# A branch on the last expert's token count picks a float32 or a split program

## The chip, the cores and the metric

The kernel runs on one core of a Trainium2 chip, in one launch. The metric is the device time in microseconds (us); three runs of the kernel before gave 1691.51, 1692.79 and 1695.13 us, median 1692.79. One more execution was profiled; the profile gives the span of that execution's instructions and the work of each engine: TensorE (PE, with its weight loads as PEld), VectorE (DVE), ScalarE (ACT), GpSimd (POOL) and SyncE (SP, whose queue issues most transfers). A "q" behind a name is that engine's instruction queue (sequencer).

## The reference, cut to what matters

Two layers of a token backbone. The first layer ends in a dense channel mixer; the second, which the change concerns, ends in a mixture of eight experts for 256 tokens of width 1024, two experts per token, hidden width 3584:

```python
def swiglu(h, w1, w3, w2):
    return (jax.nn.silu(h @ w1) * (h @ w3)) @ w2

logits = (xt @ router_w).astype(jnp.float32) + router_b.astype(jnp.float32)
top_val, top_idx = lax.top_k(logits, TOP_K)          # TOP_K = 2
gates = jax.nn.softmax(top_val, axis=-1)
# each token's row goes through its two experts:
#   out[token] += gate * swiglu(x[token], w1[e], w3[e], w2[e])
```

Then follow a gated residual, `xl + g2 * f`, and a final RMSNorm with a gain row `final_g`. All values are float32. The weights of one expert are 3 x 1024 x 3584 numbers, 42 tiles of 1 MB each; every expert's weights are read once.

## The kernel before, in words

**Places.** The eight experts are run one after the other, in eight places numbered 0 to 7. Expert 0 is always in place 0. The others are ordered at run time by their token counts (`keys`, `ranks`, `places`, lines 1204 to 1218): `RANK = (0, 7, 1, 6, 2, 5, 3, 4)` (line 823) says which rank of the order, counted from the largest, comes to which place. So place 1 has the expert with the fewest tokens, place 2 the one with the most, and place 7, the last, the one of rank 4.

**Two programs for a place.** Places in `NAT = (1, 3, 5)` run in plain float32 with room for 64 tokens: `up_nat`, `flip_nat`, `down_nat`, `scatter_nat` (lines 1341 to 1399). A 1 MB weight tile is used as it landed, and its slot is free when the last matmul that reads it has ended. All other places, the last among them, have room for 128 tokens and run split: each half tile (a chunk of 128 x 1024) is cast to a high part on ScalarE (line 135) and its remainder is made on VectorE (line 136); a product is three matmuls (`mm3`, lines 243 to 245) of high and low parts. There the slot is free when both halves have been split. The functions are `up`, `flip`, `down`, `scatter` (lines 1401 to 1465). Tokens beyond a place's room are done at the end, in a loop under the test `rv > 0` (lines 1575 to 1604), which is skipped where there are none.

**Slices.** A place has seven slices of 512 hidden columns. `up` makes silu(h w1) * (h w3), `flip` transposes it, `down` multiplies by w2 into accumulators that live through the place. The loop (lines 1516 to 1535) runs `up` of slice g, then `lower` (the `down`) of slice g - 1, then `flip` of slice g, so TensorE has other work while ScalarE and VectorE prepare the flipped operand. This holds across the border of two places too.

**Weights.** `plan` (lines 835 to 843) lists all tiles in the order of use. `w_dma` issues the next one on SP's queue as soon as a slot is free; by the time of the experts twelve slots of 1 MB rotate (four from line 90, the others added at lines 1043 to 1153). For a place whose expert is known only at run time, SP reads its number into a register first (line 1252). `w_split(n)` splits chunks ahead of use, up to five ahead; a count in `HOLD` can hold the last ones back.

**Order by hand.** The order of instructions on each engine is the order of the program text. Small work is set between by `agenda`: `plan_late(fs, at)` puts functions at numbered steps, and each weight chunk (split) or pair of weight blocks (float32) pops one step. So the routing (`gates`) runs in the first slices of place 0; `fetch`, the gather of the next place's tokens, runs inside the place before it; `scatter`, which weights a place's result by its gates and by the residual's gate row `G[1]` and adds it to the tokens, runs inside the place after it.

**The end.** In the last slice `up` has an argument `mid`: `down` of slice 54 is run between its w1 and its w3 product, and the w3 tiles come last but one in `plan`. All remaining chunks are then split, and `warm` fills TensorE with small products of ones while it waits (lines 1529 to 1538). The last scatter, the squares for the final norm (`ends`, ScalarE), the product with the gain row (POOL), the overflow test and the final scaling follow.

Of the kernel before, what the change touches and what calls it, by code (L numbers as in the profile page):

```python
# [12 lines left out]
OP = mybir.AluOpType  # L13
AX = mybir.AxisListType

P = 128
# [18 lines left out]
def tile_hybrid_headgroup_dit_moe(ctx: ExitStack, tc: tile.TileContext, a, out: bass.AP):  # L35
# [51 lines left out]
    HOLD = [0]  # L87
# [30 lines left out]
    def w_split(n):  # L118
        while st["split"] < min(n, len(chunks) - HOLD[0]):
# [701 lines left out]

    NAT = (1, 3, 5)
# [12 lines left out]
    for g in range(LAST + 2):  # L835
        if g <= LAST:
            p_moe("moe_w1", g)
            if g < LAST:
                p_moe("moe_w3", g)
        if g:  # L840
            p_moe("moe_w2", g - 1)
        if g == LAST:
            p_moe("moe_w3", g)
# [337 lines left out]
    eidx = ti[:, 8:16]  # L1181
# [4 lines left out]
    def gates():  # L1186
# [50 lines left out]
        later = [keys, ranks, places, numbers] + [lambda t=t: pick(posp[:, t], pos[:, t]) for t in range(2)] \  # L1237
# [30 lines left out]
    sn = [fa(4096 + 512 + i * 256, 256) for i in range(2)]  # L1268
    hidn = [fa(oT + 2048 + i * 256, 256) for i in range(2)]

    def gather(e, o):
        if e in NAT:
# [105 lines left out]
    def scatter_nat(ya, v, g):  # L1378
        yh, yl = ra(HS, 512), ra(HS + 512, 512)

        def weigh(hf):
            hp = slice(64 * hf, 64 * hf + 64)
            nc.vector.scalar_tensor_tensor(ya[hp], ya[hp], g[hp], G[1][hp, 512 * hf:512 * hf + 512], op0=OP.mult, op1=OP.mult)
        r = [lambda: weigh(0), lambda: weigh(1), lambda: nc.scalar.copy(yh, ya), lambda: nc.vector.tensor_sub(yl, ya, yh)]
# [16 lines left out]
    def up(e, i, h, nxt, mid=None):  # L1401
        b1, b3 = bank(), bank()
        for w, b in (("moe_w1", b1), ("moe_w3", b3)):
# [6 lines left out]
            if w == "moe_w1":  # L1410
                s = sbuf[i % 2]
                nc.scalar.activation(s, b1, AF.Silu)
                if mid is not None:
                    mid()
                    HOLD[0] = 3
# [54 lines left out]
    def fetch(e):  # L1470
        o = one_hot(e)

        def hot():
            for t, c in enumerate(list(place(e))[0]):
                if e in NAT:
# [4 lines left out]
        return [hot] + gather(e, o)  # L1480

    w_more(ra(4096, 1024), ra(5120, 1024))
    first = fetch(0)
# [5 lines left out]
    plan_late(gates(), range(2, 22))  # L1489
# [7 lines left out]
    SCAT_N = [2, 2, 6, 6, 14, 15, 18, 19, 34, 35, 38, 39]  # L1497
    ya = {}

    def lower(g):  # L1500
        e1, i1 = divmod(g, NSL)
        if i1 == 0:
            ya[e1] = bank("acc") if e1 in NAT else [bank("acc") for _ in range(2)]
        if e1 in NAT:
# [5 lines left out]
        if i1 == NSL - 1 and e1 in NAT:  # L1510
            plan_late(scatter_nat(ya.pop(e1), *sl[0]), SCAT_N)
        elif i1 == NSL - 1:
            plan_late(scatter(ya.pop(e1), *sl[0], *([HG] if g == LAST else [])),
                      SCAT if g < LAST else [0, 1, 2, 4, 5, 4, 6, 1, 2, 3, 5, 8, 6, 9])
    sl = [None]
    for g in range(LAST + 1):
        e, i = divmod(g, NSL)
        if i == 0 and e + 1 < NE:
            plan_late(fetch(e + 1), GATH if e else GATH_1)
        if e in NAT:  # L1520
            s = up_nat(e, i)
        else:
            s = up(e, i, hg[e], moe_next, (lambda: lower(g - 1)) if g == LAST else None)
        if 0 < g < LAST:
            lower(g - 1)
        if g == 0:
            plan_late([lambda s=s: hts.update({0: flip(0, s)})], [3])
        else:
            if g == LAST:
                HOLD[0] = 2  # L1530
                w_split(len(chunks))
                warm(4)
            hts[g] = flip_nat(g, s) if e in NAT else flip(g, s)
            if e in NAT and i == NSL - 1:
                w_split(st["use"] + NW[0])
    warm(7)
    HOLD[0] = 0
    lower(LAST)
# [150 lines left out]
```

## Time and profile before

| | |
|---|---|
| median of three runs | 1692.79 us (1691.51 to 1695.13) |
| the profiled execution, its time | 1693.55 us |
| its span | 1691.7 us |
| PE busy | 1636.0 us (97%), 8876 matmuls |
| DVE busy | 1147.1 us (68%) |
| ACT busy | 902.9 us (53%) |
| POOL busy | 26.2 us (2%) |
| data moved | 492.02 MB, mean 291 GB/s |
| weight tiles of the experts | 336 of 1024 KB, on SP's queue |

Rows of groups read: line of the kernel, engine, operation, what it writes and reads with its shape, how often, then busy time and the mean of one in ns, then the engine's idle time before them and what ended it. Rows of a timeline read: start in us from the span's start, duration, engine, line, operation, shapes, and in brackets the idle time before it with what ended it. Durations of matmuls overlap, since they are pipelined: the distance from start to start is what one costs. Rows of a single line read: line, engine, operation, count, then shortest, median and longest duration in ns, then the first and the last start.

### The profile page before, as it was taken

What the parts mean: (1) busy time and instruction counts of PE and PEld (TensorE: products, weight loads), DVE (VectorE), ACT (ScalarE), POOL (GpSimd) and SP (SyncE); (2) the same over time, 40 slices, a digit from 0 to 9 for tenths busy, and PEclk for the clock granted to TensorE, in tenths of its full rate; (3) what the DMA queues carried; (4) which work ended last, traced back from release to release, by engine and by line L of the source; (5) the groups of instructions that cost most, each with busy time, mean ns of one, the idle gap of its engine ahead of it and who ended that gap; (6) DMA issues with size and microseconds to landing.
All of it is one profiled execution on the core that took longest, in us unless ns stands there. A gap on an engine that the chain in (4) does not pass through costs nothing. (4 is left out here: it accounts for less than half of the span.)

```text
span 1691.7 us, 23644 instructions
## 1 busy us (share of the span) xinstructions
PE 1636.0 (97%) x8876; PEld 1268.6 (75%) x8876; DVE 1147.1 (68%) x1790; ACT 902.9 (53%) x1269; POOL 26.2 (2%) x54
## 2 busy tenths in 40 slices
PE   7999999999999999999999999999999999999996
PEld 5786788888888887978786568875588755788885
DVE  3784589966545799568983159841498513889996
ACT  4456555222225654568773157731477413777874
POOL 0101000000000010000000000000000000000001
PEclk9999899999999999999999999999999999999998
DMA  9645334665665555346999999999999999999980
GB/s 360 219 150 177 113 125 153 241 233 219 215 232 175 174 206 182 142 168 230 346 355 385 420 421 421 413 370 422 421 420 409 367 422 421 421 416 370 362 311 27
DMA packets 69226, 492.02 MB, mean 291 GB/s; under 512 B 7984, under 2 KB 8752, under 8 KB 9712
## 3 DMA queue, kind: packets, MB, share of 16 engines
q1 hardware_dynamic: 67856, 486.97, 73.8%
q0 software_dynamic: 816, 2.72, 0.7%
q8 instruction: 72, 1.18, 0.3%
q10 hardware_dynamic: 432, 0.74, 0.1%
q14 instruction: 50, 0.41, 0.1%
HBM read 489.36 MB, written 1.05 MB: 290 GB/s over the span
## 5 line engine op out<-in xcount | busy, mean ns | idle before, releaser
L136 DVE TENSOR_TENSOR RA<-FA,RA 128x1024 fp32r<-128x1024 f32 x572 | 685.2, 1226 | 157.9 <-ACT RA L135 151.6
L135 ACT CAST RA<-FA 128x1024 fp32r<-128x1024 f32 x572 | 590.7, 1051 | 278.1 <-PE mm L245 165.1
L243 PE MATMUL mm<-RA 128*128 128x512 f32 (+1 forms) x1200 | 458.6, 383 | 10.3 <-ACT RA L135 4.4
L244 PE MATMUL mm<-RA 128*128 128x512 f32 (+1 forms) x1200 | 451.7, 377 | 5.1 <-DVE RA L136 3.6
L245 PE MATMUL mm<-RA 128*128 128x512 f32 (+1 forms) x1200 | 450.6, 376 | 0.0
L243 PEld LDWEIGHTS mm<-RA 128*128 128x128 f32 x1200 | 226.9, 189 | 57.2 <-ACT RA L893 5.2
L244 PEld LDWEIGHTS mm<-RA 128*128 128x128 f32 x1200 | 227.5, 190 | 47.2 <-DVE RA L136 5.9
L245 PEld LDWEIGHTS mm<-RA 128*128 128x128 f32 x1200 | 227.2, 189 | 41.0
L243 PE MATMUL acc<-RA 128*128 128x512 f32 (+1 forms) x664 | 252.1, 380 | 3.9 <-DVE RA L765 1.8
L245 PE MATMUL acc<-RA 128*128 128x512 f32 (+1 forms) x664 | 248.0, 374 | 0.0
L244 PE MATMUL acc<-RA 128*128 128x512 f32 (+1 forms) x664 | 247.8, 373 | 0.0
L1349 PE MATMUL mm<-FA 128*64 128x256 f32 x1344 | 155.0, 382 | 0.0
L243 PEld LDWEIGHTS acc<-RA 128*128 128x128 f32 x664 | 125.5, 189 | 30.0 <-issue 3.8
L245 PEld LDWEIGHTS acc<-RA 128*128 128x128 f32 x664 | 125.3, 189 | 22.4 <-issue 0.3
L244 PEld LDWEIGHTS acc<-RA 128*128 128x128 f32 x664 | 125.6, 189 | 20.4 <-issue 0.2
L1349 PEld LDWEIGHTS mm<-FA 128*64 128x64 f32 x1344 | 92.5, 137 | 50.6 <-issue 6.8
L310 DVE SCALAR_TENSOR_TENSOR FA<-FA 128x1024 f32<-128x1024 f32 x80 | 94.5, 1222 | 7.9 <-DMA FA<-in_w_modt_dram 7.8
L1297 DVE TENSOR_TENSOR RA<-lc,RA 128x128 fp32r<-128x128 f32 x40 | 11.5, 291 | 121.7 <-ACT RA L1294 121.7
L1372 PE MATMUL acc<-FA 128*64 128x512 f32 x336 | 78.5, 597 | 0.0
L476 DVE SCALAR_TENSOR_TENSOR FA<-FA,pv 128x512 f32<-128x512 f32 (+1 forms) x128 | 74.2, 615 | 1.3 <-ACT FA L472 0.8
L1293 ACT ACTIVATE lc<-mm,modT 128x128 f32<-128x128 f32 x40 | 18.4, 460 | 84.5 <-PE mm L1288 84.5
L764 ACT CAST RA<-FA 128x256 fp32r<-128x256 f32 x44 | 17.9, 408 | 58.7 <-PE acc L245 55.9
(261 smaller groups left out, 1132.4 us busy)
## 6 DMA issues: line engine op xcount, KB each, us to landing
FA<-in_moe_w_dram SPq DMA_DIRECT2D x336, 1024.0 KB, 9.7
FA<-in_w_modt_dram SPq DMA_DIRECT2D x28, 1024.0 KB, 4.9
FA<-in_ffn_dram SPq DMA_DIRECT2D x22, 1024.0 KB, 4.8
FA<-in_ffn_w_dram SPq DMA_DIRECT2D x22, 1024.0 KB, 4.9
FA<-in_w_mod_dram SPq DMA_DIRECT2D x20, 1024.0 KB, 6.9
FA<-in_w_in_dram SPq DMA_DIRECT2D x20, 1024.0 KB, 5.0
FA<-in_w_out_dram SPq DMA_DIRECT2D x12, 1024.0 KB, 4.8
FA<-in_x_dram SPq DMA_DIRECT2D x2, 1024.0 KB, 8.6
```

The lines of the kernel that those rows point to most:

```text
L135: nc.scalar.copy(wh, raw)
L136: nc.vector.tensor_sub(wl, raw, wh)
L243: nc.tensor.matmul(ps, ll, rh, start=start, stop=False, skip_group_check=True)
L244: nc.tensor.matmul(ps, lh, rl, start=False, stop=False, skip_group_check=True)
L245: nc.tensor.matmul(ps, lh, rh, start=False, stop=stop, skip_group_check=True)
L310: nc.vector.scalar_tensor_tensor(o, raw[:, c], 1.0, csb[:, s], op0=OP.mult, op1=OP.mult, accum_out=modT[l][:, 2 * r + c, s:s + 1])
L476: nc.vector.scalar_tensor_tensor(acc, src, w, acc, op0=OP.mult, op1=OP.add)
L764: nc.scalar.copy(hh, hid(s, f))
L1293: nc.scalar.activation(v["h32"], v["b"], AF.Identity, scale=sc, bias=bi)
L1297: nc.vector.tensor_sub(h.l[:, k], v["h32"], h.h[:, k])
L1349: nc.tensor.matmul(b[64 * c:64 * c + 64, 0:256], hn[:, k], raw[:, q, 256 * c:256 * c + 256], start=k == 0, stop=k == 7, skip_group_check=True)
L1372: nc.tensor.matmul(ya[64 * hf:64 * hf + 64, :], hid[:, jj * P + 64 * r:jj * P + 64 * r + 64], raw[:, 2 * hf + jj], start=i == 0 and r == 0 ...
```

## The change

The last expert is taken out of the loop and written twice. A register is loaded with its token count, `last_n`; where it is over 64 the split program runs, otherwise a float32 program like that of places 1, 3 and 5. Both programs begin with the scatter of place 6 and end with the squares of the final norm. To make that possible:

- the place before it, place 6, gathers the last expert's tokens twice, in the split form (now at steps 9 to 38) and in the float32 form (steps 49 to 78);
- splitting stops at the last chunk of place 6 (`LIM`), so that nothing of the last expert is prepared before the branch; its transfers are still issued into free slots by `w_dma`;
- `down` of place 6's last slice is run before the branch, directly behind its own `flip`, and its w2 tiles come before the last expert's w1 tiles in `plan`;
- `HOLD`, `mid` and the `warm` calls of the last slice are gone; the last slice is a slice like the others;
- the halves of the gate row `G[1]` that float32 places need are copied once, in the routing (`gate_halves`), and `scatter_nat` weights all 128 partitions in one operation instead of two;
- the load of the final gain row is issued inside each program.

The bookkeeping of the program text (`state`, `back`) is saved ahead of the first program and restored ahead of the second.

```diff
-    HOLD = [0]
+    LIM = [None]
     def w_split(n):
-        while st["split"] < min(n, len(chunks) - HOLD[0]):
+        while st["split"] < min(n, len(chunks) if LIM[0] is None else LIM[0]):
...
     for g in range(LAST + 2):
         if g <= LAST:
...
+            ws = [("moe_w1", g), ("moe_w3", g), ("moe_w2", g - 1)]
+            if g == (NE - 1) * NSL:
+                ws = ws[2:] + ws[:2]
+            for w, h in ws:
+                if h >= 0:
+                    p_moe(w, h)
...
+            nc.vector.tensor_copy(last_n, over[:, NE - 1:NE])
...
+        def gate_halves():
+            for hf in range(2):
+                hp = slice(64 * hf, 64 * hf + 64)
+                nc.scalar.copy(gn[hp], G[1][hp, 512 * hf:512 * hf + 512])
-        later = [keys, ranks, places, numbers] + ...
+        later = [gate_halves, keys, ranks, places, numbers] + ...
...
     def raw_tile(key):
-        j = raw_j.pop(0)
+        if key[1] == NE - 1:
+            j = chunks[st["use"]][0]
+            st["use"] += 2
+        else:
+            j = raw_j.pop(0)
...
-        r = [lambda: weigh(0), lambda: weigh(1), lambda: nc.scalar.copy(yh, ya), lambda: nc.vector.tensor_sub(yl, ya, yh)]
+        r = [lambda: nc.vector.scalar_tensor_tensor(ya, ya, g, gn, op0=OP.mult, op1=OP.mult), lambda: nc.scalar.copy(yh, ya), lambda: nc.vector.tensor_sub(yl, ya, yh)]
...
+    def body(g, nat):
+        e, i = divmod(g, NSL)
+        s = up_nat(e, i) if nat else up(e, i, hg[e], moe_next)
+        if g and g - 1 in hts:
+            lower(g - 1, nat if i else e - 1 in NAT)
+        if g == 0:
+            plan_late([lambda: hts.update({0: flip(0, s)})], [3])
+        else:
+            hts[g] = flip_nat(g, s) if nat else flip(g, s)
+
     sl = [None]
-    for g in range(LAST + 1):
+    LIM[0] = [plan[j][0][1] == NE - 1 and plan[j][0][0].startswith("moe") for j, _ in chunks].index(True)
+    for g in range((NE - 1) * NSL):
         e, i = divmod(g, NSL)
+        if i == 0:
+            if e < NE - 2:
+                plan_late(fetch(e + 1, e + 1 in NAT), GATH if e else GATH_1)
+            else:
+                plan_late(fetch(e + 1, False), [0] + [9 + 4 * k + d for k in range(KD) for d in (0, 1, 1)])
+                plan_late(fetch(e + 1, True), [45] + [49 + 4 * k + d for k in range(KD) for d in (0, 1, 1)])
+        body(g, e in NAT)
+        if e in NAT and i == NSL - 1:
+            w_split(st["use"] + NW[0])
+    lower((NE - 1) * NSL - 1, False)
+    for fs in agenda:
+        run(fs)
+    del agenda[:]
...
+    def last_place(nat):
+        assert st["use"] == LIM[0] == st["split"]
+        scat(NE - 2, False)
+        if not nat:
+            LIM[0] = None
+            run(fetch(NE - 1, False)[:1])
+            w_split(st["use"] + NW[0])
+        for i in range(NSL):
+            body((NE - 1) * NSL + i, nat)
+        lower(LAST, nat)
+        nc.gpsimd.dma_start(fg, a["final_g"].to_broadcast([P, D]))
+
+        at = [0, 1, 2, 3, 4, 3, 5, 3, 6, 3, 7] if nat else [0, 1, 2, 3, 4, 3, 5, 1, 2, 3, 4, 6, 5, 7]
+        plan_late(scatter_nat(ya[NE - 1], *sl[0]) if nat else scatter(ya[NE - 1], *sl[0], HG), at)
+        plan_late([lambda t=t, hf=hf: ends(t, hf) for hf in range(2) for t in range(2)], [4, 5, 6, 7])
+        for fs in agenda:
+            run(fs)
+        del agenda[:]
...
+    ln = nc.values_load(last_n[0:1, 0:1], min_val=0, max_val=256)
+    saved, limit = state(), LIM[0]
+    with tc.If(ln > 64) as cmp:
+        last_place(False)
+    back(saved)
+    LIM[0] = limit
+    with cmp.Else():
+        last_place(True)
```

More of the change, by code (lines that the diff above doesn't have):

```diff
@@ L1236, in counts @@
             nc.vector.tensor_copy(cmax, cm)
-        later = [keys, ranks, places, numbers] + [lambda t=t: pick(posp[:, t], pos[:, t]) for t in range(2)] \
+        def gate_halves():
+            for hf in range(2):
+                hp = slice(64 * hf, 64 * hf + 64)
+                nc.scalar.copy(gn[hp], G[1][hp, 512 * hf:512 * hf + 512])
+        later = [gate_halves, keys, ranks, places, numbers] + [lambda t=t: pick(posp[:, t], pos[:, t]) for t in range(2)] \
             + [lambda t=t: pick(gtp[:, t], gt[:, t]) for t in range(2)] + [counts]
@@ L1268, in tile_hybrid_headgroup_dit_moe, with gather @@
     sn = [fa(4096 + 512 + i * 256, 256) for i in range(2)]
+    gn = fa(oT + 2560, 512)
     hidn = [fa(oT + 2048 + i * 256, 256) for i in range(2)]
-    def gather(e, o):
-        if e in NAT:
+    def gather(e, o, nat=False):
+        if nat:
             def product(k):
@@ L1468, in one_hot, with fetch @@
         return oh[e % 2]
-    def fetch(e):
+    def fetch(e, nat):
         o = one_hot(e)
@@ L1479, in hot @@
                     nc.vector.tensor_scalar(o[t], iota[:, 0:P], c, None, op0=OP.is_equal)
-        return [hot] + gather(e, o)
+        return [hot] + gather(e, o, nat)
     w_more(ra(4096, 1024), ra(5120, 1024))
-    first = fetch(0)
+    first = fetch(0, False)
     first[0]()
@@ L1496, in tile_hybrid_headgroup_dit_moe, with lower @@
     GATH_1 = [24] + [28 + 6 * k + d for k in range(KD) for d in (0, 1, 1)]
-    SCAT_N = [2, 2, 6, 6, 14, 15, 18, 19, 34, 35, 38, 39]
+    SCAT_N = [2, 6, 6, 14, 15, 18, 19, 34, 35, 38, 39]
     ya = {}
-    def lower(g):
+    def lower(g, nat):
         e1, i1 = divmod(g, NSL)
         if i1 == 0:
-            ya[e1] = bank("acc") if e1 in NAT else [bank("acc") for _ in range(2)]
-        if e1 in NAT:
+            ya[e1] = bank("acc") if nat else [bank("acc") for _ in range(2)]
+        if nat:
             down_nat(e1, i1, hts.pop(g), ya[e1])
@@ L1509, in lower, with scat @@
             sl[0] = slots(e1, one_hot(e1), list(place(e1))[1])
[L1510 to L1514, printed above, removed]
+        if i1 == NSL - 1 and e1 < NE - 2:
+            scat(e1, nat)
+    def scat(e1, nat):
+        plan_late((scatter_nat if nat else scatter)(ya[e1], *sl[0]), SCAT_N if nat else SCAT)
@@ L1545, in ends, with state, back @@
         nc.gpsimd.tensor_tensor(xg[:, t, c], xs[:, 2 + t, c], fg[:, c], op=OP.mult)
-    plan_late([lambda t=t, hf=hf: ends(t, hf) for hf in range(2) for t in range(2)], [5, 6, 8, 9])
-    for fs in agenda:
-        run(fs)
+    def last_place(nat):
[15 more added lines that the diff above has]
+        del agenda[:]
+    def state():
+        return dict(st), dict(raw_of), list(free_slots), list(wbuf), dict(hts), dict(ya), list(sl), list(raw_j)
+    def back(x):
+        for d, v in zip((st, raw_of, hts, ya), (x[0], x[1], x[4], x[5])):
+            d.clear()
+            d.update(v)
+        for l, v in zip((free_slots, wbuf, sl, raw_j), (x[2], x[3], x[6], x[7])):
+            l[:] = v
+    ln = nc.values_load(last_n[0:1, 0:1], min_val=0, max_val=256)
[6 more added lines that the diff above has]
+        last_place(True)
     raws = [fa(oR, 2048), fa(oR + 2048, 2048)]
```

43 lines of the change are left out of this document (5 added, 38 removed).

## The prediction

> **What bounds the kernel now.** I read the table by stages first, for engine and transfer load. Columns: busy us (and instructions) of TensorE, its weight load, VectorE, ScalarE, GpSimd; TensorE clock; DMA share; GB/s.
>
> ```profile
> 1250.00:1300.00 50.00, 50.00 (x230) 40.43 (x230) 43.81 (x42) 37.26 (x42) 0.00 (x0) 1.00 1.01 419
> 1550.00:1600.00 50.00, 50.00 (x228) 41.44 (x227) 47.15 (x46) 39.44 (x42) 0.00 (x0) 1.00 0.96 365
> 1600.00:1650.00 50.00, 50.00 (x230) 41.45 (x229) 47.25 (x46) 39.34 (x42) 0.55 (x1) 1.00 0.83 315
> ```
>
> In the middle of the expert mixture the transfers are the limit (419 GB/s: a 1.049 MB tile each 2.50 us). In the last place TensorE is: it never idles, while the transfers fall to 365 and 315 GB/s, held back by slots that are not free. So TensorE work removed there is time removed, until transfers limit again. The timeline gives the last place's ends: the transposes of the last slice before it, the first matmul of its own, its last.
>
> ```profile
> 1546.81 0.60 PE L1422 MATMUL mm<-ident,lc 128*128 128x128 f32 x4
> 1547.16 0.47 PE L243 MATMUL mm<-RA 128*128 128x512 f32 x1
> 1547.70 0.39 PE L245 MATMUL mm<-RA 128*128 128x512 f32 x1
> 1548.06 0.69 DVE L1426 TENSOR_TENSOR RA<-mm,RA 128x512 fp32r<-128x512 f32 x1
> 1553.62 0.39 PE L244 MATMUL mm<-RA 128*128 128x512 f32 x1
> 1675.10 0.39 PE L245 MATMUL acc<-RA 128*128 128x512 f32 x1
> ```
>
> From 1547.16 to 1675.49 the place takes 128.3 us, with the previous expert's last `down` in it. Matmuls start every 0.227 us (26 steps from 1547.70 to 1553.62). A float32 place looks so: slot transposes, the transposes of one slice, then the next slice whole.
>
> ```profile
> 1407.13 0.44 PE L1304 MATMUL mm<-ident,sel 128*128 128x128 f32 x2
> 1407.77 0.42 PE L1363 MATMUL mm<-ident,FA 128*128 128x128 f32 x2
> 1408.12 7.13 PE L1349 MATMUL mm<-FA 128*64 128x256 f32 x64
> 1415.08 3.60 PE L1372 MATMUL acc<-FA 128*64 128x512 f32 x16
> 1415.36 0.42 DVE L1357 TENSOR_TENSOR FA<-FA,mm 128x256 f32<-128x256 f32 x1 [6.85 <-PE mm L1349]
> 1418.61 0.44 PE L1363 MATMUL mm<-ident,FA 128*128 128x128 f32 x2
> 1419.14 0.37 ACT L1364 COPY FA<-mm 128x256 f32<-128x256 f32 x1 [6.92 <-PE mm L1363]
> ```
>
> 6.96 for `up`, 3.53 for `down`, 0.35 for the transposes (1407.77 to 1408.12): 10.84 us a slice.
>
> **Which program runs.** The last place takes the expert of rank 4 by count. The reference's router, on the inputs that the reference sets up, gives experts 0 to 7 counts of 25, 58, 80, 59, 50, 70, 51 and 119; expert 0 is first always, so rank 4 is expert 3 with 59. The third-best logit is nowhere closer than 0.0012 to the second, so rounding will not add six. The float32 program runs; its price is now built up.
>
> **1. Early edits.** Two ScalarE copies of half rows and a VectorE copy of a count join the routing; the copies take the step that the routing's next operation had. The stage after that step:
>
> ```profile
> 815.00:820.00 5.00, 4.13 (x17) 2.86 (x17) 4.83 (x13) 2.76 (x3) 0.00 (x0) 1.00 0.93 329
> ```
>
> I take 0: ScalarE works 2.76 of 5 us and can catch up, and the transfers, at 329 GB/s, are not yet the limit. Without that cover it is the copies' own 1.2 us (two at the 0.59 of L1451, below). One weighting instead of two saves VectorE 0.76 in three places, off the path: 0.
>
> **2. Both gathers in the sixth place.** The split one moves earlier, and a float32 one is added: eight steps of this kind.
>
> ```profile
> 830.37 0.39 PE L245 MATMUL mm<-RA 128*128 128x512 f32 x1
> 830.60 0.55 PE L1276 MATMUL mm<-sel,FA 128*128 128x64 f32 x4
> 830.96 0.48 PE L243 MATMUL mm<-RA 128*128 128x512 f32 x1
> 831.28 0.39 PE L244 MATMUL mm<-RA 128*128 128x512 f32 x1
> ```
>
> From 830.60 to 831.28 pass 0.68 where one matmul takes 0.227: 0.45 each, +3.6 us. TensorE is the limit there, so it counts whole. The moved gather keeps its count: 0. The transposes of slice 48 now end at 1547.16 + 3.6 = 1550.8.
>
> **3. The joint in front of the branch.** `down` of slice 48 no longer has `up` of the next expert before it; it needs VectorE's low half (L1426, done 1548.75): TensorE idles 1.6 us. Its 24 matmuls take 24 x 0.227 = 5.4. End: 1550.8 + 1.6 + 5.4 = 1557.8.
>
> **4. The branch.** The nearest rows are those of the overflow test, skipped at the end:
>
> ```profile
> L1575 PEldq TENSOR_LOAD <-cmax x1: 488/488/488, 1677.8 to 1677.8; - x1
> L1576 PEldq COMPARE_BRANCH x1: 3865/3865/3865, 1678.4 to 1678.4; - x1
> L1576 ACTq COMPARE_BRANCH x1: 50/50/50, 1680.8 to 1680.8; - x1
> L1576 ACTq EVENT_SEMAPHORE x2: 17/17/17, 1683.4 to 1683.5; - x2
> 1678.71 0.40 PE L1460 MATMUL mm<-RA 128*128 128x512 f32 x1
> ```
>
> TensorE's jump took 3.87 us; ScalarE, with 50 ns recorded, resumed 2.5 us later: a jump over a large body costs every engine some 2.5 to 4 us. The float32 program also lies behind the split one. Only TensorE is exposed: the others have little before the branch, since splitting stops at the place's end, and jump while TensorE does the 5.4 us of `down`. TensorE's sequencer read its register at 1677.8, 1.1 us before its last matmul gave way (1678.71 + 0.23). So the gap is 0.6 (register) + 3.9 + 0.1 (a first weight load) - 1.1 = 3.5; bounds 0 (jump hidden) and 4.9 (no lead). The place starts at 1557.8 + 3.5 = 1561.3.
> Behind the gap queue the place's first matmuls, and for the slots that they free waits SP, whose 13th tile cannot come earlier; SP's own jump is over by then.
>
> **5. The place.** TensorE alone: 7 x 10.84 = 75.9; the sixth expert's scatter, 8 matmuls, 1.8; slot transposes 0.6 (1407.13 to 1407.77); two flips that nothing covers, 1.2 together (VectorE's 0.42 product, the 0.37 copy, handoffs): 79.5 us. Transfers: twelve slots rotate (lines 90, 1043 to 1153), all full by then: their last release comes with the last split, two weight halves (12 x 0.227 = 2.7), the joint (7.0) and the gap (3.5) before the start: 13 us. The other 30 tiles need releases, the first after a quarter of `up`, 1.74 us.
>
> ```profile
> FA<-in_w_modt_dram SPq DMA_DIRECT2D x28, 1024.0 KB, 4.9
> ```
>
> An unqueued tile lands 4.9 us after issue, then one each 2.50: 1.74 + 4.9 + 29 x 2.50 = 79.1, and the last tile's half `down` 1.8: 80.9. The two limits almost meet; I take 80.9.
>
> Clock: a stalled TensorE may run slow afterwards.
>
> ```profile
> 1205.43 0.50 PE L244 MATMUL mm<-RA 128*128 128x512 f32 x1 [0.77 <-DVE RA L136]
> 1421.77 0.50 PE L244 MATMUL mm<-RA 128*128 128x512 f32 x1 [0.77 <-DVE RA L136]
> ```
>
> ```profile
> 1200.00:1210.00 10.00, 7.77 (x35) 4.77 (x32) 5.86 (x6) 7.21 (x9) 0.00 (x0) 1.00 1.01 420
> 1420.00:1430.00 10.00, 8.72 (x30) 6.85 (x31) 9.51 (x10) 7.91 (x9) 0.00 (x0) 0.83 1.01 419
> ```
>
> Behind the same stall the granted clock of the 10 us was once 1.00 and once 0.83, a loss of 1.7 us. I take half, 0.9 (bounds 0 and 3.4, both idle stretches). The last `down` ends at 1561.3 + 80.9 + 0.9 = 1643.1.
> [...]
>
> **6. The tail.**
>
> ```profile
> 1675.52 0.76 DVE L1448 SCALAR_TENSOR_TENSOR acc<-acc,gsb,FA 128x512 f32<-128x512 f32 x1 [0.60 <-PE acc L245]
> 1676.32 0.59 ACT L1451 CAST RA<-acc 128x512 fp32r<-128x512 f32 x1 [0.77 <-DVE acc L1448]
> 1677.02 0.47 PE L1459 MATMUL mm<-RA 128*128 128x512 f32 x1 [1.53 <-DVE RA L1454]
> 1677.76 2.48 DVE L1463 TENSOR_TENSOR FA<-FA,mm 128x512 f32<-128x512 f32 x4
> 1683.43 0.16 DVE L712 SCALAR_TENSOR_TENSOR small<-small 128x2 f32<-128x2 f32 x1 [3.19 <-ACTq L1576]
> ```
>
> Now 16.2 us from 1675.49 to the span's end. In the split tail one half's products run while the other half is made; float32 has one weighting, one copy, one subtraction, then products: 0.76 + 0.59 + 0.69 (as L1426) + 0.1 of handoffs + 0.74 (1677.02 to 1677.76) puts the first add 2.9 behind the last matmul, not 2.27: +0.65. The end of the new branch makes ScalarE wait for its own work before it reads the second branch's register (about 0.5, as TensorE's), which now overlaps; with handoffs +0.8. The final gain row's load, on POOL's queue, waits for a slot that falls free some ten tiles before the end and stays hidden. Tail 17.65 (16.2 to 18.5, with one more handoff at each engine).
>
> **Sum.** 1643.1 + 17.65 = 1660.8, 30.9 below the span of 1691.7. That execution took 1693.55 (0.76 above the median of 1692.79), so 1662.6 by it and 1661.9 by the median. I say 1662. All bounds taken to one side: 1655 (no gap, 79.5, clock and tail unchanged) and 1668 (1.2 early, gap 4.9, clock 3.4, tail 18.5).
>
> **The rivals.** *A, code arrives in blocks* (0.08). Per slice the float32 program has 64 + 16 + 2 matmuls and as many weight loads: 1148 instructions.
>
> ```profile
> span 1691.7 us, 23644 instructions
> q8 instruction: 72, 1.18, 0.3%
> q14 instruction: 50, 0.41, 0.1%
> L1349 PEld LDWEIGHTS mm<-FA 128*64 128x64 f32 x1344 | 92.5, 137 | 50.6 <-issue 6.8
> ```
>
> Code came in packets of 16 KB (1.18 MB in 72), 67 bytes an instruction (1.59 MB for 23644): 77 KB, so four packets beyond the first. If each stalled like the jump, 4 x 3.87 = 15.5: 1677. Against it: three whole float32 places waited 6.8 us in all for "issue", for nothing that the profile shows. [...]
>
> *B, transfers are thinner than taken* (0.10): if 30 tiles come at the 365 GB/s of the 1550 row (2.87 us each), 29 x 0.37 = 10.7 more: 1673. For it: the place is held by transfers by my own sum. Against: 365 is what free slots allowed, 419 what the queue can do.
>
> *C, the jump is hidden* (0.07): the 3.5 and the slow clock vanish: 1657.5. For it: ScalarE's branch record of 50 ns. Against: ScalarE worked again only 2.5 us later.
>
> *D, slower: the split program runs* (0.05), from 65 tokens on. It pays +3.6 for the second gather, 1.6 at the joint, some 1.1 for the branch, 0.9 clock, 0.8 at the second branch, and the float32 gain is absent: about 8.0, 1701. Against it: 59.
>
> **How the numbers follow.** Forecast 0.68 with its own 1655 to 1668. To leave no more than 2 in 10 out I go to 1654 below and 1675 above, which takes in C and B; A and D stay out. A measurement here tells 0.2%, 3.4 us, from no change. Forecast, A, B and C are all faster: 0.93. Slower 0.05 (D); the 0.02 left, for what I do not see, goes to same.
>
> **What would show it.** Right: the native forms of L1349's and L1372's matmuls go from 21 slices to 28, the split ones fall by 504; a TensorE gap of 3 to 4 us near 1558; float32 slices of 10.8 to 11.7 us with transfers near 420 GB/s; the span's last 17 to 18 us unchanged in kind. Wrong: split matmuls still run behind the branch (D); repeated gaps in the place that no transfer ends (A); transfer waits at nearly every tile (B).

## The result, and the profile after

The changed kernel takes 1666.46 us (median of 4 runs, 1663.17 to 1667.76); beside it, on the same chip, the kernel before took 1692.15 (4 runs, 1691.43 to 1695.13). The ratio is 0.9842, with a 95% interval of 0.9823 to 0.9861: 26 us faster, 23 to 30. Forecast were 1662, with 1654 to 1675 as the range. The profiled execution took 1667.13 us, its span is 1665.4.

From the page of the kernel after, the span and five groups of matmuls:

```profile
span 1665.4 us, 23501 instructions
...
L243 PE MATMUL mm<-RA 128*128 128x512 f32 (+1 forms) x1088 | 416.2, 383 | 9.2 <-ACT RA L135 4.4
...
L243 PE MATMUL acc<-RA 128*128 128x512 f32 (+1 forms) x608 | 230.3, 379 | 5.3 <-DVE RA L765 1.8
...
L1361 PE MATMUL mm<-FA 128*64 128x256 f32 x1792 | 206.2, 382 | 3.6 <-DMA FA<-in_moe_w_dram 2.7
...
L1384 PE MATMUL acc<-FA 128*64 128x512 f32 x448 | 104.5, 597 | 1.8 <-DMA FA<-in_moe_w_dram 1.1
```

The float32 `up` has 1792 matmuls, 28 slices of 64 (21 before, x1344), and the split matmuls of line 243 fall by 112 and 56: the float32 program ran, for the expert with 59 tokens. New is the last item of the last two rows: TensorE waits for weight tiles, 2.7 and 1.1 us.

From its timeline, TensorE around the branch and through the place:

```profile
1552.76 0.60 PE L1428 MATMUL mm<-ident,lc 128*128 128x128 f32 x4
1554.76 0.50 PE L243 MATMUL acc<-RA 128*128 128x512 f32 x1 [1.40 <-DVE RA L1432]
...
1560.11 0.39 PE L245 MATMUL acc<-RA 128*128 128x512 f32 x1
1561.40 7.13 PE L1361 MATMUL mm<-FA 128*64 128x256 f32 x64 [0.91 <-issue]
...
1633.62 1.95 PE L1361 MATMUL mm<-FA 128*64 128x256 f32 x16 [1.91 <-DMA FA<-in_moe_w_dram]
1636.19 1.95 PE L1361 MATMUL mm<-FA 128*64 128x256 f32 x16 [0.63 <-DMA FA<-in_moe_w_dram]
1638.79 1.94 PE L1384 MATMUL acc<-FA 128*64 128x512 f32 x8 [0.65 <-DMA FA<-in_moe_w_dram]
1641.18 1.94 PE L1384 MATMUL acc<-FA 128*64 128x512 f32 x8 [0.46 <-DMA FA<-in_moe_w_dram]
...
1646.12 1.94 PE L1384 MATMUL acc<-FA 128*64 128x512 f32 x8 [0.17 <-SPq L1620]
```

The joint is as forecast: 1.40 us of idle time for VectorE's low half, then 24 matmuls. The gap at the branch is 0.91, not 3.5. The place runs from 1561.40 to 1648.06 (1646.12 + 1.94), 86.7 us, not 81.8, and four of its last six tiles come with TensorE waiting for them, 3.65 us in all (1.91, 0.63, 0.65, 0.46). The branch itself, from the rows of its two lines:

```profile
L1585 PEldq TENSOR_LOAD <-ti x1: 491/491/491, 1556.3 to 1556.3; - x1
...
L1587 PEldq COMPARE_BRANCH  x1: 4367/4367/4367, 1556.9 to 1556.9; - x1
```

TensorE's sequencer read the register at 1556.3, 4.0 us before the last matmul of the joint gave way (1560.11 + 0.23 = 1560.34), and came out of the jump at 1561.3. The jump is 0.5 us longer than what was taken from the overflow test (3.87), and most of it lies under the joint's own matmuls.

The transfers, from the table by stages (columns: busy us and instructions of TensorE, its weight load, VectorE, ScalarE, GpSimd; TensorE clock; DMA share; GB/s), and SP's issues from 1558 on:

```profile
1556.00:1558.00 2.00, 2.00 (x10) 1.66 (x9) 0.00 (x0) 0.00 (x0) 0.00 (x0) 1.00 1.00 422
1558.00:1560.00 2.00, 2.00 (x11) 1.65 (x10) 0.76 (x1) 0.00 (x0) 0.00 (x0) 1.00 0.14 45
1560.00:1562.00 2.00, 1.09 (x9) 0.61 (x9) 0.00 (x1) 0.00 (x0) 0.00 (x0) 1.00 0.00 0
1562.00:1564.00 2.00, 2.00 (x22) 1.59 (x19) 0.00 (x0) 0.00 (x0) 0.00 (x0) 1.00 0.03 8
1564.00:1566.00 2.00, 2.00 (x22) 1.60 (x20) 0.00 (x0) 0.82 (x2) 0.00 (x0) 1.00 0.76 250
...
1586.00:1596.00 10.00, 10.00 (x74) 5.01 (x68) 1.11 (x2) 0.85 (x3) 0.00 (x0) 1.00 1.01 419
```

```profile
L102 SPq DMA_DIRECT2D FA<-in_moe_w_dram x31: 332/333/343, 1563.4 to 1624.9; - x31
```

From 1558.2 or so all slots hold tiles that nobody has used yet, and the queues stand still for 6 us; then 31 tiles are issued, each behind a release. The place needs 42, so 11 slots rotate, not 12. The granted clock stays 1.00.

### The profile page after: what moved, and what is told of

It reads as the page before. It is cut to its first block, busy times and chain, and to the rows that moved or that the text cites. A ratio compares the mean times of both kernels' runs of the same rounds, so it can differ in the third digit from the quotient of the medians.

```text
span 1665.4 us, 23501 instructions
## 1 busy us (share of the span) xinstructions
PE 1601.3 (96%) x8928; PEld 1214.4 (73%) x8928; DVE 1041.6 (63%) x1697; ACT 817.7 (49%) x1194; POOL 26.5 (2%) x54
## 5 line engine op out<-in xcount | busy, mean ns | idle before, releaser
L136 DVE TENSOR_TENSOR RA<-FA,RA 128x1024 fp32r<-128x1024 f32 x488 | 587.1, 1226 | 155.2 <-ACT RA L135 149.6
L135 ACT CAST RA<-FA 128x1024 fp32r<-128x1024 f32 x488 | 503.6, 1051 | 261.6 <-PE mm L245 157.9
L243 PE MATMUL mm<-RA 128*128 128x512 f32 (+1 forms) x1088 | 416.2, 383 | 9.2 <-ACT RA L135 4.4
L244 PE MATMUL mm<-RA 128*128 128x512 f32 (+1 forms) x1088 | 409.1, 376 | 5.5 <-DVE RA L136 3.8
L245 PE MATMUL mm<-RA 128*128 128x512 f32 (+1 forms) x1088 | 408.1, 375 | 0.0
L243 PEld LDWEIGHTS mm<-RA 128*128 128x128 f32 x1088 | 207.0, 191 | 52.0 <-ACT RA L135 5.1
L244 PEld LDWEIGHTS mm<-RA 128*128 128x128 f32 x1088 | 207.1, 190 | 43.4 <-DVE RA L136 6.3
L243 PE MATMUL acc<-RA 128*128 128x512 f32 (+1 forms) x608 | 230.3, 379 | 5.3 <-DVE RA L765 1.8
L245 PEld LDWEIGHTS mm<-RA 128*128 128x128 f32 x1088 | 206.8, 190 | 37.0
L245 PE MATMUL acc<-RA 128*128 128x512 f32 (+1 forms) x608 | 226.1, 372 | 0.0
L244 PE MATMUL acc<-RA 128*128 128x512 f32 (+1 forms) x608 | 225.9, 372 | 0.0
L1361 PE MATMUL mm<-FA 128*64 128x256 f32 x1792 | 206.2, 382 | 3.6 <-DMA FA<-in_moe_w_dram 2.7
L1361 PEld LDWEIGHTS mm<-FA 128*64 128x64 f32 x1792 | 124.6, 137 | 71.3 <-issue 12.5
L243 PEld LDWEIGHTS acc<-RA 128*128 128x128 f32 x608 | 114.9, 189 | 29.2 <-issue 3.8
L245 PEld LDWEIGHTS acc<-RA 128*128 128x128 f32 x608 | 114.9, 189 | 20.2 <-issue 0.3
L244 PEld LDWEIGHTS acc<-RA 128*128 128x128 f32 x608 | 115.0, 189 | 18.2 <-issue 0.2
L1384 PE MATMUL acc<-FA 128*64 128x512 f32 x448 | 104.5, 597 | 1.8 <-DMA FA<-in_moe_w_dram 1.1
L1384 PEld LDWEIGHTS acc<-FA 128*64 128x64 f32 x448 | 30.4, 137 | 50.6 <-issue 42.4
```

The source lines that it names most:

```text
L135: nc.scalar.copy(wh, raw)
L136: nc.vector.tensor_sub(wl, raw, wh)
L243: nc.tensor.matmul(ps, ll, rh, start=start, stop=False, skip_group_check=True)
L244: nc.tensor.matmul(ps, lh, rl, start=False, stop=False, skip_group_check=True)
L245: nc.tensor.matmul(ps, lh, rh, start=False, stop=stop, skip_group_check=True)
L1361: nc.tensor.matmul(b[64 * c:64 * c + 64, 0:256], hn[:, k], raw[:, q, 256 * c:256 * c + 256], start=k == 0, stop=k == 7, skip_group_check=True)
```

## The experiments

A profiled execution differs from the next one ahead of the branch already: with the same program up to there, the joint (the first matmul of the split `down`) began at 1551.60 to 1555.88 us. So stretches are compared: from the joint to the place's first float32 matmul, the place up to the end of its last matmul, and the tail from there to the span's end.

| kernel | time, median us | joint to place | place | tail |
|---|---|---|---|---|
| the changed kernel | 1666.46 | 6.6 | 86.7 | 17.3 |
| no branch | 1666.40 | 5.7 | 86.9 | 17.7 |
| twelfth slot rotates | 1659.83 | 6.6 | 83.8 | 17.0 |
| two more slots | 1664.17 | 8.8 | 83.8 | 16.9 |
| float32 program fallen into | 1667.64 | 5.7 | 87.1 | 20.3 |
| both of these | 1664.38 | 5.7 | 83.4 | 20.2 |
| count known late | 1670.30 | 10.2 | 88.3 | 17.5 |
| gather in the split program | 1660.72 | 6.0 | 86.8 | 17.7 |
| gain row early | 1664.75 | 6.1 | 85.9 | 17.8 |

**The branch taken out.**

```diff
-    with tc.If(ln > 64) as cmp:
-        last_place(False)
-    back(saved)
-    LIM[0] = limit
-    with cmp.Else():
-        last_place(True)
+    last_place(True)
```

> The changed kernel with its float32 program for the last place in a straight line: same order, both gathers, same joint, no branch (the split program for more than 64 tokens is left out). Theory: TensorE's sequencer reaches the branch about 4 us before TensorE runs dry, so that only 1.0 us of the branch shows at the start of the place and 0.8 at its end; both go: 1664.5 to 1666 against 1666.5. The prediction's account (3.5 of gap and 0.8 behind): 1662. Third account (the branch's far side costs the whole excess of the place, 4.9 us): 1660 to 1661, and the TensorE waits for transfers at the end of the place are gone.

1666.40 (4 runs, 1662.21 to 1667.86; ratio to before 0.9831, 0.9803 to 0.9859). The place begins 1.0 us sooner behind the joint and is as long:

```profile
1554.57 0.50 PE L243 MATMUL acc<-RA 128*128 128x512 f32 x1 [1.40 <-DVE RA L1432]
...
1632.85 1.95 PE L1361 MATMUL mm<-FA 128*64 128x256 f32 x16 [1.72 <-DMA FA<-in_moe_w_dram]
...
1643.06 4.02 PE L1384 MATMUL acc<-FA 128*64 128x512 f32 x16 [0.52 <-ACT FA L1376]
```

The prediction's 3.5 of gap falls, and so does any account in which the far side of the branch makes the place long: without a branch it still waits 1.72 us for the same tile. The tail kept its length too: the 0.8 laid to the new branch there is not to be seen.

**The twelfth slot.** One slot (the 2048 columns of `FA` at 6144) is added in line 1045 when its old use is over, but equals an entry of `kept`, the list of slots that `release` does not give back. It takes one tile and is lost, before and after the change, so that eleven slots rotate where twelve were said. The edit takes the entry out.

```diff
+    del kept[-1]
     free_slots.append(fa(4096 + 2048, 2048))
```

> The changed kernel in which the twelfth buffer for weight tiles comes back into rotation when it is released; so far it is used once and then lost, because it compares equal to an entry of the list of buffers that are not returned. Theory: in the last place 30 tiles instead of 31 are still to come after the first release, at 2.50 us each: the place is 2.5 shorter, 84.2 instead of 86.7, and the whole 2 to 3 shorter: 1664. Upstream an additional tile in flight may add up to 1 us of gain. Rival (the place is bound by TensorE or by the far side of the branch): 1666.5, same length of the place.

1659.83 (4 runs, 1657.67 to 1660.2; 0.9794, 0.977 to 0.9818), the place 83.8, and 30 tiles to come:

```profile
L102 SPq DMA_DIRECT2D FA<-in_moe_w_dram x30: 332/333/343, 1559.4 to 1617.9; - x30
```

One slot more, 2.8 us less: the place hangs on its transfers at 2.5 us a tile, as the theory has it. The median fell by 6.6; nearly all of the other 3.8 lies ahead of the branch (in the profile the joint begins 4.0 sooner), where profiled executions with the same program differ by as much, and the intervals of the two ratios nearly touch. Whether the slot gains anything there stays open.

**Two more slots at the branch.**

```diff
+        else:
+            free_slots.extend([fa(6144, 2048), fa(oT, 2048)])
+            w_dma()
         for i in range(NSL):
```

> The changed kernel in which, at the head of the float32 program, two more buffers join the rotation (the lost twelfth one and the gathered expert's source rows, no longer needed by this program; the program for experts over their bound, which does not run with these counts, would need those rows and is so left out of what is right). Two tiles load in the idle time of the queues around the branch. Theory: 29 tiles instead of 31 to come after the first release, 5.0 us less by transfers, 81.7 for the place; TensorE's own 79.5 to 80.5 is then nearly the bound: 1661.5 to 1663, and the waits of TensorE for weight tiles at the end of the place shrink to under 1 us in all. Rival: 1666.5 and the waits stay.

1664.17 (4 runs, 1662.68 to 1667.15; 0.9821, 0.9797 to 0.9845), 2.3 less where 3.5 to 5 were expected. The waits for tiles are nearly gone, but something new stands in front of the place: a branch record, a timeline row and four stages of this kernel:

```profile
L1590 PEldq COMPARE_BRANCH  x1: 6534/6534/6534, 1558.0 to 1558.0; - x1
```

```profile
1564.69 8.81 PE L1361 MATMUL mm<-FA 128*64 128x256 f32 x64 [3.08 <-issue]
```

```profile
1562.00:1564.00 2.00, 0.00 (x0) 0.00 (x0) 0.00 (x0) 0.00 (x0) 0.00 (x0) 1.00 1.02 410
1564.00:1566.00 2.00, 1.31 (x8) 0.97 (x10) 0.00 (x0) 0.00 (x0) 0.00 (x0) 0.70 0.47 188
1566.00:1568.00 2.00, 2.00 (x12) 1.40 (x10) 0.00 (x0) 0.00 (x0) 0.00 (x0) 0.50 0.01 4
1568.00:1570.00 2.00, 2.00 (x20) 1.64 (x18) 0.00 (x0) 0.00 (x0) 0.00 (x0) 0.94 0.43 66
```

The jump took 6.5 us instead of 4.4 while the transfers ran on at 410 GB/s; TensorE stood 3.08 us, and its clock fell to 0.70 and 0.50, so that the first 64 matmuls took 8.81 instead of 7.13. 2.2 of gap and 1.7 of clock are what is missing. Whether the jump or the additional issues make the gap, the next two runs take apart.

**The float32 program fallen into.** The order of the two programs is turned, alone, and then together with the two slots.

```diff
-    with tc.If(ln > 64) as cmp:
-        last_place(False)
+    with tc.If(ln < 65) as cmp:
+        last_place(True)
...
-        last_place(True)
+        last_place(False)
```

> The changed kernel with the two programs in the other order: the float32 program stands first and is fallen into, the split program is jumped to. In the run with the bound at 32, where the split program is fallen into, TensorE's compare-and-branch took 86 ns; where the float32 program is jumped to it took 4367. Theory (the long record is the fetch of the jump's target): TensorE's record falls to about 0.1 us, the gap of 0.9 at the start of the place is gone; but the place's end hangs on the transfers, whose restart comes about 1 us earlier with its start: 1665 to 1666.5, E' 1 us earlier. Rival (the record waits for the value or for the matmuls before it, whichever program follows): the record stays above 3 us. Third account (the float32 program's own code was late throughout, and this made the place long): the place falls by 3 or more, 1662 or less.

> The two additional buffers at the head of the float32 program, and the float32 program fallen into. With the buffers alone TensorE's jump took 6.5 us instead of 4.4, the gap grew to 3.1 us and the granted clock fell to 0.7 and 0.5 for 4 us behind it. Theory (the fetch of the jump's target is a transfer that queues with the weight tiles that the two buffers start): without a jump taken the gap is under 0.3, the clock stays at 1.00, and the two tiles give what they are worth, 5 us less by transfers and TensorE's 80 as the new bound: 1659 to 1661. Rival (the gap of 3.1 comes from the additional issues and their waits, not from the jump): gap and clock as with the buffers alone, 1664.

Alone 1667.64 (4 runs, 1666.35 to 1669.41; 0.9857, 0.9842 to 0.9872); with the two slots 1664.38 (4 runs, 1658.75 to 1665.16; 0.9824, 0.9805 to 0.9842). The branch and the tail of the turned kernel:

```profile
L1587 PEldq COMPARE_BRANCH  x1: 86/86/86, 1553.7 to 1553.7; - x1
```

```profile
1656.32 0.16 DVE L712 SCALAR_TENSOR_TENSOR small<-small 128x2 f32<-128x2 f32 x1 [6.46 <-ACTq L1620]
```

Where the branch is not taken its record is 86 ns, in the middle of the same matmuls: the 4.4 us are the jump, not a wait for the value. With the two slots the gap is gone and the clock stays at 1.00 (first row 7.13 long, as in the changed kernel), so the gap of 3.08 came from the jump and not from the additional issues. What the jump spends its time on, a fetch in both theories, was the author's guess and no run shows it. From the joint to the place's end the two slots now give 3.7 us (89.0 against the 92.7 of the turned kernel without them), not 5; the place itself is 83.4, where one slot more had 83.8, so the second slot is worth little. Both times missed what was expected because of the other end: the program that is fallen into must jump over the other when it is done (3.49 us in TensorE's record), ScalarE goes through that jump and the overflow test's one behind the other, and VectorE waits 6.46 us for it instead of 3.56. The tail is 3 us longer. What the turn takes from the head it loses at the end.

**The count known late.** The count is written by an operation that reads the accumulator in which the joint's `down` ends.

```diff
+    last_f = cp.tile([P, 1], F32, name="last_f")
...
-            nc.vector.tensor_copy(last_n, over[:, NE - 1:NE])
+            nc.vector.tensor_copy(last_f, over[:, NE - 1:NE])
...
     lower((NE - 1) * NSL - 1, False)
+    nc.vector.scalar_tensor_tensor(last_n, ya[NE - 2][1][:, 511:512], 0.0, last_f, op0=OP.mult, op1=OP.add)
     for fs in agenda:
```

> The changed kernel in which the count for the branch is written only by an operation of VectorE that reads the last column of the accumulator that the last split down ends in; what is computed is the same. The engines can read it only once TensorE is done. Theory (the jump costs TensorE its 4.4 us and is hidden in the changed kernel because the sequencer runs 4 us ahead of the matmuls): the whole jump shows, with a handoff and the register's load, 0.5 each: a gap of 5 to 5.5 at the start of the place in place of 0.9, and after it a clock loss of 0 to 1.7: 1670.5 to 1673. Rival (the record is long only because TensorE is busy): gap 1.5 to 2, 1667 to 1668.

1670.30 (4 runs, 1667.58 to 1673.94; 0.9864, 0.9849 to 0.988):

```profile
L1589 PEldq COMPARE_BRANCH  x1: 3507/3507/3507, 1562.7 to 1562.7; - x1
```

```profile
1566.33 9.62 PE L1362 MATMUL mm<-FA 128*64 128x256 f32 x64 [4.50 <-issue]
```

With no matmul left to cover it the whole jump shows: a gap of 4.50, then 2.5 us of clock (9.62 against 7.13), 5.3 in all from the joint to the place's end; the place's transfer bound takes some of it. What hides the jump in the changed kernel is the sequencer's lead of 4.0 us.

**The split gather moved into the split program.**

```diff
-                plan_late(fetch(e + 1, False), [0] + [9 + 4 * k + d for k in range(KD) for d in (0, 1, 1)])
-                plan_late(fetch(e + 1, True), [45] + [49 + 4 * k + d for k in range(KD) for d in (0, 1, 1)])
+                plan_late(fetch(e + 1, True), GATH)
...
-            run(fetch(NE - 1, False)[:1])
+            run(fetch(NE - 1, False))
```

> The changed kernel in which the gather for the split program is made inside that program, so that with a count of 59 only the float32 gather runs, at the sixth place's ordinary steps. Theory (the second gather delays TensorE by 4.0 us in a place that TensorE sets): the joint comes 4.0 earlier, the place keeps its 86.7, 1662.5. The prediction's size: 3.6 earlier, 1662.9. Rival (the sixth place is set by its casts or its weight tiles, and a gather less is hidden): 1666.5, and the joint where it was.

1660.72 (4 runs, 1657.93 to 1663.16; 0.9802, 0.9771 to 0.9834). The sixth place's first Silu and the joint, first of the changed kernel, whose joint stands above at 1554.76, then of this one:

```profile
1430.89 0.60 ACT L1421 ACTIVATE lc<-mm 128x512 f32<-128x512 f32 x1 [0.30 <-PE mm L245]
```

```profile
1430.86 0.60 ACT L1421 ACTIVATE lc<-mm 128x512 f32<-128x512 f32 x1 [0.21 <-PE mm L245]
...
1550.91 0.50 PE L243 MATMUL acc<-RA 128*128 128x512 f32 x1 [1.40 <-DVE RA L1432]
```

123.9 against 120.1: the second gather costs 3.8 us, whole, in a place that TensorE sets. The median says 5.7, with an interval that holds 3.8.

**The gain row early.** Its load goes to the free columns at 6144, ahead of the branch.

```diff
-    fg, xg, sq, ss = fa(0, D), ...
+    fg, xg, sq, ss = fa(6144, D), ...
+    nc.gpsimd.dma_start(fg, a["final_g"].to_broadcast([P, D]))
     def ends(t, hf):
...
         lower(LAST, nat)
-        nc.gpsimd.dma_start(fg, a["final_g"].to_broadcast([P, D]))
```

> The changed kernel with the final gain row's load (512 KB) put ahead of the branch and into memory that is free by then, so that it no longer runs among the last weight tiles. Theory (it takes 512 KB at 420 GB/s, 1.25 us, from the tiles on which the place's end hangs): the place 85.4 instead of 86.7, 1665.2. Rival (its transfer is hidden): place 86.7, 1666.5.

1664.75 (4 runs, 1662.64 to 1669.43; 0.9841, 0.9809 to 0.9873): no difference that the times can tell. In the profile the place is 85.9, 0.8 less, and the longest wait for a tile falls from 1.91 to 0.55:

```profile
1631.29 1.95 PE L1361 MATMUL mm<-FA 128*64 128x256 f32 x16 [0.55 <-DMA FA<-in_moe_w_dram]
```

The direction is the theory's, the size two thirds of it. Places with the same tiles and slots differ by 0.4 from one profile to another (86.7 to 87.1 in the table), so the 0.8 is a rough figure.

**The other program (more than 32 tokens).** The bound at 32 sends the 59 tokens through the split program.

```diff
-    with tc.If(ln > 64) as cmp:
+    with tc.If(ln > 32) as cmp:
```

> The changed kernel with the branch's bound at 32 instead of 64, so that the count of 59 takes the split program. Theory: the split program pays only what the change adds around it: second gather 4.0, joint 1.4, a gap at the branch of about 1, second branch 0.8, so about 7 over the kernel before: 1697 to 1701. Rival (code of a branch's far side arrives late and in blocks): the split program, which has more instructions, pays several us at intervals too: 1705 or more, with repeated waits for issue behind the branch. Second rival (the two programs hardly differ and the gain is elsewhere): about 1666.

1703.08 (5 runs, 1702.24 to 1704.51), 1.0055 times before (1.0036 to 1.0075): 9.3 us slower, 6 to 13. Its branch is not taken (TensorE's record 86 ns) and nothing waits for "issue" behind it, so the far side is not what it pays. Three things were not in the expected 7: the wait of the place's first flip, the clock behind it, and the wait of the last `down`:

```profile
1571.78 0.79 PE L1428 MATMUL mm<-ident,lc 128*128 128x128 f32 x4 [2.05 <-DVE lc L1422]
...
1678.62 0.50 PE L243 MATMUL acc<-RA 128*128 128x512 f32 x1 [1.40 <-DVE RA L1432]
```

```profile
1572.00:1574.00 2.00, 2.00 (x8) 1.69 (x7) 0.69 (x1) 1.40 (x2) 0.00 (x0) 0.54 0.95 332
```

The first flip of the place has no `down` ahead of it any more, which now sits before the branch: 2.05 us. Behind it the granted clock falls to 0.54, and to 0.60 in the two us after these, which costs 1.7. The last `down`, without `mid` and `warm`, waits 1.40 for VectorE as the joint does. The expected gap of 1 at the branch did not come. In the profiles this kernel is 10.6 us longer than the one before (spans of 1702.3 and 1691.7): 4.3 ahead of the joint's transposes, 4.6 from there to the end of the last `down`, 1.7 in the tail. The four terms of the middle (1.40 at the joint, 2.05, 1.7, 1.40) make 6.5, so about 2 come back there in a way that was not taken apart.

**A better version, in two steps.** The first has the twelfth slot, the float32 program fallen into, the split gather inside the split program, the gain row at the float32 program's head, and the sixth place's last `down` inside both programs, in the float32 one behind the first `up` (`g0` is the last expert's first slice, `u` the first chunk of that `down`).

```diff
-    lower((NE - 1) * NSL - 1, False)
     for fs in agenda:
...
+            if nat and i == 0:
+                st["use"] = LIM[0]
+                s = up_nat(NE - 1, 0)
+                v, st["use"] = st["use"], u
+                lower(g0 - 1, False)
+                st["use"] = v
+                scat(NE - 2, False)
+                hts[g0] = flip_nat(g0, s)
+            else:
+                body(g0 + i, nat)
```

> A version from what the runs showed: the lost buffer back in rotation; the float32 program fallen into; the branch ahead of the sixth place's last down, so that in the float32 program the first up of the last place covers the handoff of the flip and frees buffers 5 us earlier; the split gather inside the split program; the final gain row loaded at the head of the float32 program into memory that it does not use. Theory: from the 1659.8 of the twelve buffers alone, gather 3.9, joint 1.4, gap 0.9 and the place's excess over TensorE's own 80, 3.8, go: 1650. Rival (the transfers take back what the order gives, since the place then begins with fewer idle queues before it but the same 42 tiles of 2.50 us, and the upstream float32 place is bound by them too): 1654 to 1656.

1655.64 (5 runs, 1652.83 to 1657.88; 0.9781, 0.9766 to 0.9796), not 1650. The last `down` ended at 1632.60 with one wait of 0.36 for a tile left, but the tail was 21.3, with VectorE waiting for ScalarE's two jumps:

```profile
1645.60 0.16 DVE L712 SCALAR_TENSOR_TENSOR small<-small 128x2 f32<-128x2 f32 x1 [7.14 <-ACTq L1638]
```

So the second step makes one decision of two: the value is the last count plus 256 times the largest excess, and the last operations stand in both programs.

```diff
+            nc.vector.scalar_tensor_tensor(last_n, cm, 256.0, lf, op0=OP.mult, op1=OP.add)
...
     with tc.If(ln < 65) as cmp:
         last_place(True)
+        finish()
...
     with cmp.Else():
         last_place(False)
+        overflow()
+        finish()
```

> The better version, with one decision in place of two: the branch's value is the last count plus 256 times the largest excess, the float32 program with the kernel's last operations is fallen into, and the split program, the program for experts over their bound and the same last operations are jumped to. Theory (in the version before, ScalarE's jumps from the program's end and past the overflow program, 3.2 and 2.9 us, stood in the tail between its last square sum and VectorE's step that needs to know it): the tail goes from 21.3 to 15; the one jump at the end runs while the output is written: 1649 to 1650. Rival (VectorE's step waits for GpSimd's last product or for the sums, not for the jumps): 1655.6. Third account (the end of the program waits for the last jump behind the output): 1651 to 1653.

1650.26 (5 runs, 1648.89 to 1652.19; 0.9744, 0.9718 to 0.9769): 43 us faster than before, 16 faster than the changed kernel. From its timeline, the last `down` and the tail:

```profile
1628.76 3.94 PE L1387 MATMUL acc<-FA 128*64 128x512 f32 x16 [0.52 <-ACT FA L1379]
...
1636.65 4.92 POOL L1560 TENSOR_TENSOR FA<-FA,lc 128x512 f32<-128x512 f32 x4 [89.29 <-DVE FA L1409]
...
1639.05 0.16 DVE L712 SCALAR_TENSOR_TENSOR small<-small 128x2 f32<-128x2 f32 x1 [0.84 <-ACT FA L1559]
1639.24 1.14 DVE L233 TENSOR_SCALAR ti<-small 128x2 int32<-128x2 int32 x1
...
1640.41 1.19 DVE L235 TENSOR_SCALAR small<-ti 128x2 int32<-128x2 int32 x1
...
1644.62 0.36 ACTq L1667 DMA_DIRECT2D out_dram<-FA  x1
```

No wait for a tile is left, nor one for a jump: VectorE goes on 0.84 us behind its own last work, at once after ScalarE's sum. The tail is 17.7, not the 15 expected: two small integer operations take 1.14 and 1.19 us where they took 0.17 in the kernels whose GpSimd was done by then, and from the last issue to the span's end pass 5.8 us (1644.62 to 1650.4; 4.7 in the changed kernel, 1660.73 to 1665.4). Whether that end waits for the program's last jump was not taken apart.

The same version with its bound at 32 shows what the other side pays for it.

> The same version with the branch's bound at 32, so that the split program, with its own gather in front, is jumped to. Theory: what the other side of the decision costs now: from the 1703 of the changed kernel with its bound at 32, the sixth place's gathers give back about 4 of the second and 4 of the first, the twelfth buffer up to 4 upstream, while the gather inside the program stands bare in front of it, 24 matmul steps with a copy each, 8 to 12, and the jump and the uncovered splits of the first weight halves 4 to 6: 1703 to 1710.

1706.43 (3 runs, 1705.64 to 1708.0; 1.0079, 1.0051 to 1.0107): 13 us slower than before for a last expert with more than 64 tokens.

## Why the prediction was right, and where it was not

The time fell in the range and the sign was right, by a sum in which two errors cancelled and a third stayed; that it came as near as 4.5 us to the forecast is in part luck. By its steps:

1. **Early edits**, 0 forecast: 0.64, inside its bound of 1.2, but not where the copies run. The Silus of the first four slices of place 0, before and then after, there with the two copies:

```profile
786.89 0.60 ACT L1412 ACTIVATE lc<-mm 128x512 f32<-128x512 f32 x1
...
798.36 0.60 ACT L1412 ACTIVATE lc<-mm 128x512 f32<-128x512 f32 x1
...
814.13 0.60 ACT L1412 ACTIVATE lc<-mm 128x512 f32<-128x512 f32 x1 [0.38 <-PE mm L245]
...
834.01 0.60 ACT L1412 ACTIVATE lc<-mm 128x512 f32<-128x512 f32 x1 [0.33 <-PE mm L245]
```

```profile
788.18 0.60 ACT L1421 ACTIVATE lc<-mm 128x512 f32<-128x512 f32 x1
...
799.66 0.60 ACT L1421 ACTIVATE lc<-mm 128x512 f32<-128x512 f32 x1
...
802.05 1.25 ACT L1243 COPY FA<-FA 64x512 f32<-64x512 f32 x2
...
815.33 0.60 ACT L1421 ACTIVATE lc<-mm 128x512 f32<-128x512 f32 x1 [0.30 <-PE mm L245]
...
835.85 0.60 ACT L1421 ACTIVATE lc<-mm 128x512 f32<-128x512 f32 x1 [0.32 <-PE mm L245]
```

   The copies lie between the second and the third Silu, and that stretch is no longer than before (15.67 after 15.77): ScalarE's free time did cover them. The stretch behind it went from 19.88 to 20.52 (835.85 - 815.33). In it the last steps of the routing now run on VectorE, 1.7 to 1.9 us later against the third Silu, and TensorE's longest wait for VectorE's split grew from 0.87 to 1.04; that the moved steps cost the 0.64 fits this, but no run takes them out. The first Silu is 1.3 later already, ahead of every changed line.
2. **Both gathers**, +3.6 forecast: 3.8. Right; TensorE was the limit, and the experiment that moved one of them away says so.
3. **The joint**, 1.6 and 5.4 forecast: 1.40 and 5.6. Right. That it ended at 1560.3 and not 1557.8 comes mostly from steps 1 and 2 (0.8 of it) and from the start that was 1.3 later.
4. **The branch**, gap 3.5 forecast: 0.91. The price of the jump was right (4.37 against 3.87), the lead was not: 1.1 us was read off the overflow test, where TensorE's few last matmuls each wait for something, while at the joint the sequencer ran 4.0 us ahead. Rival C, given 0.07, is nearly what happened here. The place began at 1561.40, a tenth of a microsecond from forecast, by luck: this error took up the one of step 3.
5. **The place**, 80.9 and 0.9 for the clock forecast: 86.7 and 0. The step that failed. That transfers would hold it, not TensorE, was right; their sum was short. Twelve slots were counted from the lines that add them, and the test in `release` that drops one again was not read: one tile, 2.5 (2.8 by experiment). The gain row was called hidden, although it runs among the last weight tiles (issued at 1625.5, landed 8.4 us later): 0.8 of place by experiment, 1.25 by its size. The remaining 1.8 to 2.5 is spread and was not taken apart: the first release came 1.98 behind the start (1.74 taken), and behind it the queues moved 250, 385 and 369 GB/s in three stages of 2 us from 1564 on before they passed 410. TensorE alone is 81 (83.4 less 2.2 of waits, 1.0 for a tile and 1.2 put down to SP's queue, in the run with two more slots and no jump), 79.5 was taken; it does not bind. Most of that difference is the scatter of place 6: its 8 matmuls, set in four pairs among the others, lengthen the place by 3.3, not 1.8 (the `up` with the first pair in it takes 7.78, from 1569.41 to 1577.19, instead of 6.96; four times 0.82). The clock stayed at 1.00 in every stage of the place, behind gaps of 1.40 and 0.91; in the runs with gaps of 3.08 and 4.50 it cost 1.7 and 2.5, and 1.7 behind the 2.05 of the split program. Length alone does not decide: in the kernel before, waits of 1.46 and 0.77 with one matmul between them left the clock at 1.00 at 1206 us and brought it to 0.58 at 1422. What else does, no run shows.
6. **The tail**, 17.65 forecast: 17.3. Right in its first term, the first add 3.0 behind the last matmul (2.9 forecast, 2.27 before). The 0.8 for the new branch is not shown: the run without a branch has 17.7.

**The rivals.** A (code arrives in blocks, each with a stall) is refuted: no gap but one, and as long a place without any branch. B (thin transfers at 365 GB/s) is refuted by the 419 GB/s of the place; it named the right limit with a wrong reason. D did not happen with 59 tokens; forced, it cost 9.3 us, where 8.0 was worked out. The sums agree better than their terms: the gap at the branch was not there, while two flips that lost their cover, 2.05 and 1.40, were not in the 8.0, and the clock cost 1.7 instead of 0.9.

## What to carry to other kernels

When a sum says that two limits nearly meet, as 79.5 and 80.9 did, check every transfer that runs beside the weight tiles (the gain row's cost 0.8 us of the place) and count the buffers that really rotate, in the trace (tiles issued behind a point, against tiles needed: 31 against 42), not in the code. The branch cost TensorE here its jump less the work already queued ahead of it: a jump of 4.37 us, begun 3.5 before the joint's last matmul gave way, showed as a gap of 0.91; one of 3.51 with no such lead stood whole in a gap of 4.50. So put a branch where the sequencer has a few microseconds of lead, and let the likely path fall through (0.09 us here), but look at what the jump at its end then delays (a tail 3 us longer here). Work moved across the branch uncovered its neighbours on both sides, 1.40 us at the joint and 2.05 at the first flip of the split program.

## What was not expected of the hardware

- A jump on TensorE's sequencer ahead of the place took 3.51 us with the count known late (10 GB/s in the 4 us around it), 4.37 in the changed kernel (transfers that fell from 422 GB/s to 0 meanwhile) and 6.53 with two more slots (410 GB/s in the last 2 us before the place began). The same branch not taken took 0.09. At the end of the program, over the overflow program, it was 3.87 in the kernel before and 3.34 in the changed one. That transfers lengthen a jump is not shown: one run has the 6.53.
- VectorE's two integer operations of 128x2 took 1.14 and 1.19 us while GpSimd multiplied, 0.17 when it had finished; the float32 operation between them took 0.15. What makes them longer was not tested further.
